# Low parts on VectorE, two weight pieces ahead and a later turn of the last queries, at the end of attention in a two-layer trunk

## The chip, the cores and the metric

One core of one Trainium2 chip. The metric is the device time of one execution in microseconds; before the change three runs gave 866.49, 868.11 and 872.79 us, median 868.11 us. Engines are named as in the profile: PE (matmul; PEld is its weight load), DVE, ACT, POOL, and SP, which issues most of the loads.

## The reference

640 tokens of width 1024 (512 latent, 128 context) pass two layers: gated grouped-query attention (16 query heads, 4 key heads of 64) and a gated linear recurrence in both directions. What matters here is the end of layer 0 and what its modulation needs:

```python
sh_s, sc_s, g_s = _adaln(c, ada_w[i], ada_b[i])      # SiLU(c) @ ada_w[i] + ada_b[i], cut in three
q = _rms_norm(q.reshape(B, L, N_HEADS, HEAD_DIM), q_gain)
...
p = jax.nn.softmax(s, axis=-1)
return jnp.einsum('bkgqs,bskd->bqkgd', p, vf).astype(q.dtype)
...
gated = o.reshape(B, L, ATTN_WIDTH).astype(jnp.float32) * jax.nn.silu(g.astype(jnp.float32))
return gated.astype(o.dtype) @ w_out
...
xs = _layer_norm(DEEPNORM_ALPHA * xs + g_s * out_s, ln_gain[i], ln_bias[i])
```

## The kernel before, in words

**High and low parts.** Products of activations and weights are made from two fp32r parts of each operand: the high part is a rounded copy made on ACT, the low part the difference of the value and its high part, made by one subtraction on DVE or POOL. A product is then three matmuls: high by high, high by low, low by high. `split_piece` (L220) does this for a weight piece of 128x1024 (ACT copy L225, subtraction L226 on the engine that it is given), `split_act` (L947) for one of the eight 128x640 slices of the gated attention output `gs` (copy L948 into `hhi`, subtraction L949 into `hlo`).

**Loads.** Weight pieces of 512 KB come in one fixed `order` (L370 to L384), issued by `pump` (L199) on SP so that at most `RAW_AHEAD = 5` pieces are loaded and not yet split, in a ring of six buffers. In that order the seven last adaLN chunks (`ADA_B[3]`, two pieces each) come first, and then the eight pieces of attention's output weight `attn_w_out` (two column halves nh of four pieces i).

**Attention's weave.** `att_gen` sweeps four key heads ("chunks" c of 4 query heads and 256 columns). Of each unit (one head, 256 queries) the front makes scores on PE (`sc`, L732 and L733), their negated maximum on DVE (`nm`, L826), the exponential with its sum on ACT (`p`, L829), and two steps later the reciprocal on DVE (`rc`, L833) and the scaling on POOL (`p`, L834). Two units later the back turns p on PE (`pt`, L841), copies it out of PSUM (`pts`, L737, on ACT and DVE), and multiplies by the values (`pot`, L759), which DVE gates into `gs` (L764). A second generator runs beside it, one step for every 0.85 of its steps at most (`weave`, `Side`): the next chunk's queries (`q_gen`, L600: projection `qmm`, root mean square, rotary tables, high and low part `qs` on ACT and DVE, turn by PE `qps` L589, copy into X), mixed with adaLN chunks (`adaps` L266; row to columns L289; sums into `shsc` and `gcol` on DVE, L297 and L300). Behind chunk 3's queries stand, in this order: the last seven adaLN chunks (once chunk 3's backs have begun), the first two pieces of the output weight (`prefetch_gen`, L959), and the split of the first six slices of `gs` (`split_gs(range(6))`). All this stands in one block whose instructions a list scheduler reorders within each engine.

**After the block** (L993 on, in program order save for what the code marks with `high_priority` or pins): the split of the last two slices (L1067), the other six output weight pieces (L1069), the first recurrence weights (`rhi`, `rlo`), and then the output projection `outp` (L1005, L1008, L1009) of five token tiles in the order (0,0), (1,0), (0,1), (1,1), (2,0) and so on of (tile, column half), 24 matmuls each. Both halves of one tile lie in one PSUM tile of two banks. After each half, `Norm.part` (L1026) reads it on DVE: a product with the gate (`y`, L1030), the residual (L1031), statistics (L1033).

The low parts stand on these engines before: `qs` and the recurrence's weights on DVE; `hlo` on POOL (L953); output weight pieces in turn, even i on POOL and odd i on DVE (L944).

Of the kernel before, what the change touches and what calls it, by code (L numbers as in the profile page):

```python
# [132 lines left out]
def hybrid_step(ctx: ExitStack, tc: tile.TileContext, a: dict, o: dict):  # L133
    nc = tc.nc
# [62 lines left out]
    order = deque()  # L197
# [22 lines left out]
    def split_piece(hi, lo, src, lo_eng=None, pinned=False):  # L220
        pump()
        got, raw = ahead.popleft()
        assert got == src, (got, src)
        pin = tc.keep_in_program_order if pinned else lambda ins: ins
        pin(nc.scalar.copy(hi, raw))  # L225
        pin((lo_eng or nc.gpsimd).tensor_tensor(lo, raw, hi.bitcast(F32), ALU.subtract))  # L226
        pump()
# [84 lines left out]
    def ada_gen(chunks):  # L312
        todo, last = None, None
        for l, c in chunks:
            ps = bank1("adaps")
            both = [take((f"ada_w{l}", c, i)) for i in range(2)]
            for i in (1, 0):
                ada_part(ps, i, both[i], 1)
            yield
            if last:  # L320
                last()
            last = todo and ada_out(*todo)
            yield
            todo = (l, c, ada_row(ps))
        if last:
            last()
        if todo:
            last = ada_out(*todo)
            yield
            if last:  # L330
                last()
                yield
# [25 lines left out]
    def pieces(name, c, n=2):  # L358
        return [(name, c, i) for i in range(n)]

    PIECES = [(nh, i) for nh in range(2) for i in range(4)]
# [5 lines left out]
    def ada_pieces(part):  # L367
        return [p for l, c in part for p in pieces(f"ada_w{l}", c)]
# [4 lines left out]
    for c in range(3):  # L373
        order.extend(pieces("attn_w_in", c + 1))
        order.extend(ada_pieces(ADA_B[c]))
    order.extend(ada_pieces(ADA_B[3]))
    order.extend(("attn_w_out", nh, i) for nh, i in PIECES)
    order.extend(("rec_w_in", h, i) for h in range(RH) for i in range(5))
    order.extend(("rec_w_out", nh, i) for nh, i in OUT1)
    for n, back in ((0, 2), (1, 1)):  # L380
# [17 lines left out]
    hhi = hp.tile([P, KT, NT], F32R, tag="hhi", name="hhi")  # L398
    hlo = hp.tile([P, KT, NT], F32R, tag="hlo", name="hlo")
# [100 lines left out]
    gs = gsp.tile([P, KT, NT], F32, tag="gs", name="gs")  # L500
# [76 lines left out]
    def q_split(r, tt0, n, odd, X, alloc):  # L577
        s2 = prep.tile([P, 1024], F32R, tag="s2", name="qs2", bufs=2)
        rv = view(r, 0, [[HD, 4 * n], [1, HD]])
        hv = view(s2, HD * odd, [[P, 4 * n], [1, HD]])  # L580
        nc.scalar.copy(hv, rv)
        nc.vector.tensor_tensor(view(s2, HD * (1 - odd), [[P, 4 * n], [1, HD]]), rv, hv.bitcast(F32), ALU.subtract)

        def back(i):
            pt = alloc("qps")
            pr = pt[:].bitcast(F32R)
            for h in range(4):
                s = i * 512 + h * P
                nc.tensor.transpose(pr[:, h * P:(h + 1) * P], s2[:, s:s + P], identr)  # L589
            c0 = (tt0 + i) * P  # L590
            nc.scalar.copy(X[:, :, c0:c0 + P], pt[:].rearrange("p (a b) -> p a b", a=4))  # L591
        return back
# [7 lines left out]
    def q_gen(c, X):  # L600
        w = Weights("attn_w_in", c, (nc.vector, nc.vector))
        yield
        yield
        pend = None
        for tt0, n in UNITS:
            ps = yield from tok_unit(w, tt0, n, "qmm")
            rstd = rms_stat(ps, n)
            yield
            if pend:
                for i in range(pend[1]):  # L610
                    pend[0](i)
                    yield
            else:
                yield
            yield
            qn = rms_apply(ps, n, rstd)
            r = rope_apply(qn, tt0, n, cosq, sinq, qg)
            yield
            pend = (q_split(r, tt0, n, c % 2, X, bank1), n)
        yield  # L620
        for i in range(pend[1]):
            pend[0](i)
            yield
# [191 lines left out]
    back_of = [0]  # L815
# [95 lines left out]
    side = Side()  # L911
# [27 lines left out]
    def wo_gen(layer, pieces, wpool):  # L939
        for nh, i in pieces:  # L940
            hi = wpool.tile([P, 1024], F32R, tag=f"wohi{nh}{i}", name="wohi")
            lo = wpool.tile([P, 1024], F32R, tag=f"wolo{nh}{i}", name="wolo")
            wo[nh, i] = tuple(t[:].rearrange("p (k n) -> p k n", k=2) for t in (hi, lo))
            split_piece(hi, lo, ("attn_w_out" if layer == 0 else "rec_w_out", nh, i), (nc.gpsimd, nc.vector)[i % 2])  # L944
            yield

    def split_act(dst_hi, dst_lo, src, eng=None):  # L947
        nc.scalar.copy(dst_hi, src)  # L948
        (eng or nc.vector).tensor_tensor(dst_lo, src, dst_hi.bitcast(F32), ALU.subtract)  # L949

    def split_gs(ks):
        for k in ks:
            split_act(hhi[:, k, :], hlo[:, k, :], gs[:, k, :], nc.gpsimd)  # L953
            yield

    ws = ExitStack()
# [2 lines left out]
    def prefetch_gen():  # L959
        wb.close()  # L960
        pq.close()
        wr.append(lpool("wr", 2))
        woa.append(ws.enter_context(pool("woa", 1)))
        yield from wo_gen(0, PIECES[:2], woa[0])

    def q_next(c):
        Xs[c] = xq[c % 2].tile([P, 4, NT], F32R, tag="X", name=f"X{c}")
        yield from q_gen(c, Xs[c])

    def mixed(q, ada):  # L970
        owed = 0.0
        for _ in q:
            yield
            owed += MIX
            while owed >= 1.0:
                owed -= 1.0
                if next(ada, True) is None:
                    yield
        yield from ada

    for c in range(1, 4):
        side.items.append((f"q{c}", mixed(q_next(c), ada_gen(ADA_B[c - 1])), lambda c=c: front_of[0] >= c - 1))
    side.items.append(("a", ada_gen(ADA_B[3]), lambda: back_of[0] == 3))
    side.items += [("w", prefetch_gen()), ("s", split_gs(range(6)), lambda: back_of[0] == 3)]
    weave(att, side, SIDE_B)
    side.finish()
    ph.close()
# [226 lines left out]
    norms = {}  # L1214
    for tt, nh in ((0, 0), (1, 0), (0, 1), (1, 1), (2, 0), (2, 1), (3, 0), (3, 1), (4, 0), (4, 1)):
        if nh == 0:
            norms[tt] = Norm(0, tt)
        out_mms(norms[tt].ps[nh], tt, nh, hhi, hlo)
        norms[tt].part(nh, norms[tt].ps[nh])
        if nh == 1:  # L1220
            with tc.high_priority() if tt == TS else nullcontext():
                norms[tt].finish()
            if tt > 1:
                h1_tile(tt - 1, norms[tt - 1].y)
            elif tt == 1:
                h1_tile(0, norms[0].y)
# [267 lines left out]
    side = Side(("t", tail_gen()))  # L1494
# [9 lines left out]
    for tt in range(TT):  # L1504
# [7 lines left out]
        else:  # L1512
            w = D // parts
            for n in range(parts):
                nh, c = divmod(n * w, 512)
# [86 lines left out]
```

## Time and profile before

| | |
|---|---|
| median of three runs | 868.11 us (866.49 to 872.79) |
| the profiled execution's own time | 868.67 us |
| its span, first to last instruction | 866.9 us, 19259 instructions |
| PE busy | 827.0 us (95%) |
| DVE / ACT / POOL busy | 528.8 / 382.5 / 205.9 us |
| mean granted TensorE clock | 0.992 |
| chain that ended last | PE 83%, DVE 5%, ACT 4%, issue 4%, DMA 3%, POOL 1% |

A busy row gives microseconds and share of the span. A row of waits names the engine and line that stood idle, behind what, for how long in all, how often and the longest. A timeline row gives start, duration, engine, line, operation, output and inputs, shape and count, and in brackets the idle time before it with what ended it; equal instructions in a row are merged, and a merged matmul's duration is the time from its first start to its last end. A row of windows gives the stretch in us, busy time (and instructions) of PE, PEld, DVE, ACT and POOL, the granted clock of TensorE (1.00 is full), the share of DMA and GB/s.

### The profile page before, as it was taken

The numbers are of one execution on the slowest core, as the hardware profiler recorded it, in microseconds if no ns is written. First come the engines' busy times: TensorE is split into PE (matmuls) and PEld (weight loads), VectorE is DVE, ScalarE is ACT, GpSimd is POOL, SyncE is SP. The second block draws the span as 40 slices with busy tenths as digits, with TensorE's granted clock in tenths as the row PEclk, the third lists the DMA queues.
The fourth block names the chain that finished last, engine by engine and source line by source line (L and its number), as shares of the span: only waits on it lengthen the run. The fifth ranks groups of instructions, "written<-read, shape, count | busy, mean of one in ns | idle before, by whom it ended". The sixth has DMA issues, their size and how long they took to land.

```text
span 866.9 us, 19259 instructions
## 1 busy us (share of the span) xinstructions
PE 827.0 (95%) x8124; PEld 739.7 (85%) x8124; DVE 528.8 (61%) x942; ACT 382.5 (44%) x756; POOL 205.9 (24%) x247
## 2 busy tenths in 40 slices
PE   5989999999999898989999999999999999999996
PEld 3669999778778766667899999999999999998886
DVE  3447535665846664567635666675848495867558
ACT  2222536554745754503244444444443454544332
POOL 0113001413414743600000040323324040502011
PEclk9999999999999999999999999999999999999999
DMA  9922112212212046251221232232224232322023
GB/s 358 411 88 86 55 68 74 99 50 99 98 49 99 1 161 229 88 228 74 83 73 50 82 96 83 79 105 70 85 68 123 62 99 81 98 74 93 8 97 122
DMA packets 29606, 89.86 MB, mean 104 GB/s; under 512 B 4336, under 2 KB 8944, under 8 KB 28496
## 3 DMA queue, kind: packets, MB, share of 16 engines
q1 hardware_dynamic: 19728, 73.08, 23.8%
q0 software_dynamic: 3168, 9.31, 3.9%
q10 hardware_dynamic: 6624, 6.24, 2.3%
q8 instruction: 64, 1.05, 0.5%
q14 instruction: 22, 0.18, 0.1%
HBM read 79.44 MB, written 9.18 MB: 102 GB/s over the span
## 4 chain that ended last, share of the span: by engine, by line
PE 83%; DVE 5%; ACT 4%; issue 4%; DMA 3%; POOL 1%; SPq 0%; ACTq 0%; DVEq 0%; POOLq 0%
PE rps L1147 7%; PE rps L1149 7%; PE rps L1148 6%; PE vgps L1137 5%; PE vgps L1139 4%; PE vgps L1138 4%; PE pot L759 4%; PE pt L841 4%; PE outp L1005 3%; PE outp L1009 2%; PE outp L1008 2%; PE adaps L266 2%; PE gps L337 2%; PE lv L1285 2%; PE gps L338 2%
## 5 line engine op out<-in xcount | busy, mean ns | idle before, releaser
L1147 PE MATMUL rps<-h1hi,rhi 128*128 128x320 f32 x368 | 118.3, 321 | 0.0
L1148 PE MATMUL rps<-h1lo,rhi 128*128 128x320 f32 x368 | 113.5, 308 | 0.0
L1149 PE MATMUL rps<-h1hi,rlo 128*128 128x320 f32 x368 | 113.4, 308 | 0.0
L226 DVE TENSOR_TENSOR rlo<-raw,rhi 128x1024 fp32r<-128x1024 f32 x32 | 44.1, 1380 | 46.0 <-ACT rhi L225 46.0
L834 POOL TENSOR_SCALAR p<-p,rc 128x640 f32<-128x640 f32 x64 | 53.2, 836 | 78.5 <-DVE rc L833 68.9
L1147 PEld LDWEIGHTS rps<-h1hi,rhi 128*128 128x128 f32 x368 | 69.2, 188 | 1.3
L1148 PEld LDWEIGHTS rps<-h1lo,rhi 128*128 128x128 f32 x368 | 69.3, 188 | 0.0
L1149 PEld LDWEIGHTS rps<-h1hi,rlo 128*128 128x128 f32 x368 | 69.1, 188 | 0.1
L829 ACT ACTIVATE p<-sc,nm 128x640 f32<-128x640 f32 x64 | 51.1, 799 | 35.4 <-DVE nm L826 29.1
L826 DVE TENSOR_REDUCE nm<-sc 128x1 f32<-128x640 f32 x64 | 51.6, 817 | 18.6 <-PE sc L733 17.9
L225 ACT CAST rhi<-raw 128x1024 fp32r<-128x1024 f32 x32 | 33.6, 1050 | 61.0 <-PE rps L1148 57.1
L1258 ACT COPY kc<-A 128x640 f32<-128x640 f32 x40 | 32.4, 811 | 52.0 <-PE lv L1285 29.7
L841 PE MATMUL pt<-ident,p 128*128 128x128 f32 x320 | 50.6, 283 | 3.2 <-ACT pts L737 1.5
L1137 PE MATMUL vgps<-rhi,h1hi 128*128 128x256 f32 x180 | 51.2, 284 | 0.0
L1138 PE MATMUL vgps<-rlo,h1hi 128*128 128x256 f32 x180 | 50.5, 280 | 0.0
L1139 PE MATMUL vgps<-rhi,h1lo 128*128 128x256 f32 x180 | 50.2, 279 | 0.0
L737 ACT COPY pts<-pt 128x512 f32<-128x512 f32 x64 | 36.6, 588 | 27.8 <-PE pt L841 27.5
L841 PEld LDWEIGHTS pt<-ident,p 128*128 128x128 f32 x320 | 37.7, 146 | 12.5 <-issue 8.9
L194 POOL TENSOR_TENSOR rstdo<-rs_t,mhalf 128x5 f32<-128x5 f32 x8 | 9.5, 1192 | 162.3 <-DVE rs_t L193 162.3
L732 PE MATMUL sc<-kk,X 128*128 128x320 f32 x128 | 42.8, 344 | 2.9 <-ACT p L829 2.8
L1137 PE MATMUL vgps<-wspare,h1hi 128*128 128x256 f32 x140 | 41.5, 297 | 0.0
L337 PE MATMUL gps<-hhi,whi 128*128 128x320 f32 x128 | 40.1, 313 | 0.7 <-ACT X L591 0.4
(273 smaller groups left out, 2413.2 us busy)
## 6 DMA issues: line engine op xcount, KB each, us to landing
raw<-in_rec_w_in SPq DMA_DIRECT2D x40, 512.0 KB, 4.0
raw<-in_ada_w SPq DMA_DIRECT2D x32, 512.0 KB, 3.9
raw<-in_ada_w SPq DMA_DIRECT2D x8, 1024.0 KB, 10.8
raw<-in_attn_w_in SPq DMA_DIRECT2D x16, 512.0 KB, 4.7
raw<-in_attn_w_out SPq DMA_DIRECT2D x8, 512.0 KB, 5.9
raw<-in_rec_w_out SPq DMA_DIRECT2D x8, 512.0 KB, 3.7
h<-in_xT SPq DMA_DIRECT2D x8, 320.0 KB, 9.2
x1d<-y SPq DMA_DIRECT2D x5, 512.0 KB, 2.6
```

Of the source, the lines that this page charges most:

```text
L226: pin((lo_eng or nc.gpsimd).tensor_tensor(lo, raw, hi.bitcast(F32), ALU.subtract))
L337: nc.tensor.matmul(ps[:, :320], w.hi(k)[:, c], hhi[:, k, t], start=(k == 0), stop=False)
L826: nc.vector.tensor_reduce(nm[:, 0:1], sc[:, :, :320], AX.XY, ALU.max, negate=True)
L829: nc.scalar.activation(halves(p[:]), sc[:, :, :320], AF.Exp, bias=nm[:, 0:1], accum_out=su[:, 0:1])
L834: nc.gpsimd.tensor_scalar(p, p, rs[:, 0:1], 1.0, ALU.mult, ALU.mult)
L841: nc.tensor.transpose(pt[:, i * 256 + q * P:i * 256 + (q + 1) * P], ps[q][:, (k0 + i) * P:(k0 + i + 1) * P], ident)
L1137: nc.tensor.matmul(out, h1hi[:, k, t], hi, start=(k == 0), stop=False)
L1138: nc.tensor.matmul(out, h1hi[:, k, t], lo, start=False, stop=False)
L1139: nc.tensor.matmul(out, h1lo[:, k, t], hi, start=False, stop=(k == KT - 1))
L1147: nc.tensor.matmul(ps[:, j, :320], hi[:, k, :], h1hi[:, k, t], start=(k == 0), stop=False)
L1148: nc.tensor.matmul(ps[:, j, :320], hi[:, k, :], h1lo[:, k, t], start=False, stop=False)
L1149: nc.tensor.matmul(ps[:, j, :320], lo[:, k, :], h1hi[:, k, t], start=False, stop=(k == KT - 1))
```

## The change

The edits, all around the end of attention:

- `wo_gen` gives every low part of a weight piece to DVE, and `split_gs` gives `hlo` to DVE. With that POOL makes no low part any more: four pieces of `wolo` and eight of `hlo` go over.
- In the load order the first two output weight pieces stand ahead of the last seven adaLN chunks, and the generator that splits them (`prefetch_gen`) runs ahead of these chunks too, right behind chunk 3's queries.
- `q_gen` yields twice more ahead of the turn of its last unit, in chunks 1 to 3.
- `Norm.part` of the first two token tiles is issued with high priority.

```diff
     for c in range(3):
         order.extend(pieces("attn_w_in", c + 1))
         order.extend(ada_pieces(ADA_B[c]))
+    order.extend(("attn_w_out",) + p for p in PIECES[:2])
     order.extend(ada_pieces(ADA_B[3]))
-    order.extend(("attn_w_out", nh, i) for nh, i in PIECES)
+    order.extend(("attn_w_out",) + p for p in PIECES[2:])
...
             pend = (q_split(r, tt0, n, c % 2, X, bank1), n)
+        yield
+        yield
         yield
...
-            split_piece(hi, lo, ("attn_w_out" if layer == 0 else "rec_w_out", nh, i), (nc.gpsimd, nc.vector)[i % 2])
+            split_piece(hi, lo, ("attn_w_out" if layer == 0 else "rec_w_out", nh, i), nc.vector)
...
-            split_act(hhi[:, k, :], hlo[:, k, :], gs[:, k, :], nc.gpsimd)
+            split_act(hhi[:, k, :], hlo[:, k, :], gs[:, k, :])
...
+    side.items.append(("w", prefetch_gen()))
     side.items.append(("a", ada_gen(ADA_B[3]), lambda: back_of[0] == 3))
-    side.items += [("w", prefetch_gen()), ("s", split_gs(range(6)), lambda: back_of[0] == 3)]
+    side.items += [("s", split_gs(range(6)), lambda: back_of[0] == 3)]
...
-        norms[tt].part(nh, norms[tt].ps[nh])
+        with tc.high_priority() if tt < 2 else nullcontext():
+            norms[tt].part(nh, norms[tt].ps[nh])
```

What this does to the order of DVE's instructions at three places follows (in the rows of the change, lines after L617 carry numbers up to five higher).

DVE from the last gating of attention to the first sums of the output projection, before (`pot` is the product of probabilities and values, `wolo` and `rlo` are low parts of output and recurrence weights, `y` of the outp row is the gated output of tile 0):

```order
L764 TENSOR_TENSOR gs<-pot,gs 128x256
L993 UNCONDITIONAL_BRANCH
L226 TENSOR_TENSOR wolo<-raw,wohi 128x1024 x3
L226 TENSOR_TENSOR rlo<-raw,rhi 128x1024
L1074 TENSOR_TENSOR modA<-shsc_85,lnc 128x16
L1075 TENSOR_TENSOR modB<-shsc_85,lnc 128x16
L226 TENSOR_TENSOR rlo<-raw,rhi 128x1024
L1076 TENSOR_TENSOR modB<-modB,shsc_85 128x16
L1030 TENSOR_TENSOR y<-outp,gate_108 128x512
```

The same place with the change:

```order
L767 TENSOR_TENSOR gs<-pot,gs 128x256
L997 UNCONDITIONAL_BRANCH
L952 TENSOR_TENSOR hlo<-gs,hhi 128x640
L226 TENSOR_TENSOR wolo<-raw,wohi 128x1024
L952 TENSOR_TENSOR hlo<-gs,hhi 128x640
L226 TENSOR_TENSOR wolo<-raw,wohi 128x1024 x5
L1034 TENSOR_TENSOR y<-outp,gate_108 128x512
L1078 TENSOR_TENSOR modA<-shsc_85,lnc 128x16
L1079 TENSOR_TENSOR modB<-shsc_85,lnc 128x16
L226 TENSOR_TENSOR rlo<-raw,rhi 128x1024
```

Two `hlo` and three more `wolo` came in, and the first read of `outp` moved ahead of both recurrence weights.

DVE in the last adaLN chunks, some 25 us earlier, before (`row` and `gcol` are an adaLN chunk's sums as a row and as columns):

```order
L764 TENSOR_TENSOR gs<-pot,gs 128x256
L280 COPY row<-adaps 128x256
L226 TENSOR_TENSOR wolo<-raw,wohi 128x1024
L826 TENSOR_REDUCE nm<-sc 128x1 x2
L300 TENSOR_TENSOR gcol_83<-adaps_3794,small 128x4
```

With the change:

```order
L767 TENSOR_TENSOR gs<-pot,gs 128x256
L280 COPY row<-adaps 128x256
L829 TENSOR_REDUCE nm<-sc 128x1 x2
L300 TENSOR_TENSOR gcol_83<-adaps_3814,small 128x4
L280 COPY row<-adaps 128x256
```

The low part of the output weight piece is gone from between the row and the maxima.

DVE while chunk 3's last queries are made, before (`qs` is the low part of the queries, `ss` the sum of their squares):

```order
L826 TENSOR_REDUCE nm<-sc 128x1
L833 RECIPROCAL rc<-su 128x1
L297 TENSOR_TENSOR shsc_85<-adaps_3231,small 128x4
L826 TENSOR_REDUCE nm<-sc 128x1
L582 TENSOR_TENSOR qs_3203<-r,qs_3203 128x8x64
```

With the change:

```order
L829 TENSOR_REDUCE nm<-sc 128x1
L952 TENSOR_TENSOR hlo<-gs,hhi 128x640
L836 RECIPROCAL rc<-su 128x1
L952 TENSOR_TENSOR hlo<-gs,hhi 128x640
L297 TENSOR_TENSOR shsc_85<-adaps_3231,small 128x4
L952 TENSOR_TENSOR hlo<-gs,hhi 128x640 x2
L829 TENSOR_REDUCE nm<-sc 128x1
L583 TENSOR_TENSOR qs_3203<-r,qs_3203 128x8x64
```

Four low parts of `gs` stand between two maxima that followed each other with two short instructions between them. A little later two `wolo`, with another `hlo` ahead of them, stand around the maximum of chunk 3's context scores, and on ACT the two high parts of these pieces stand behind the copy of the last turned queries and ahead of two copies `pts`.

## The prediction

> **What bounds the kernel now.** I read the busy times first, then PE's waits around the change, then the stretches of 4 us in which these fall, and then the rows of each wait in order of time. The first row of the page:
>
> ```profile
> PE 827.0 (95%) x8124; PEld 739.7 (85%) x8124; DVE 528.8 (61%) x942; ACT 382.5 (44%) x756; POOL 205.9 (24%) x247
> ```
>
> PE is busy for 827.0 of 866.9 us, so only its idle time, about 40 us, and time at a lower clock can be won. PE's waits between 270 and 420 us, the stretch that the change touches:
>
> ```profile
> PE outp L1005 <- DVE y L1030: 4.2, 2, 3.8
> PE qps L589 <- DVE qs L582: 2.7, 1, 2.7
> PE adaps L289 <- DVE gcol L300: 2.6, 1, 2.6
> PE sc L732 <- ACT p L829: 0.9, 4, 0.3
> PE outp L1005 <- DVE gs L764: 0.5, 1, 0.5
> ```
>
> Three waits, all for DVE, make most of it: 2.7 us for the last queries, 2.6 us for adaLN columns, 3.8 us for the first sums of the output projection. The windows (columns: stretch, busy PE, PEld, DVE, ACT, POOL, clock, DMA):
>
> ```profile
> 284.00:288.00 4.00, 3.92 (x34) 3.67 (x32) 1.79 (x5) 4.00 (x9) 4.00 (x4) 1.00 0.00 0
> 296.00:300.00 4.00, 1.67 (x17) 1.69 (x17) 1.81 (x5) 2.47 (x7) 2.85 (x3) 1.00 0.01 4
> 332.00:336.00 4.00, 2.20 (x25) 1.23 (x23) 2.37 (x3) 1.60 (x3) 2.15 (x1) 1.00 0.87 300
> 338.38:341.78 3.40, 3.40 (x17) 3.36 (x18) 1.10 (x3) 1.30 (x3) 0.79 (x2) 0.50 0.87 310
> 368.00:372.00 4.00, 0.23 (x2) 0.17 (x2) 3.97 (x7) 0.00 (x0) 0.64 (x1) 1.00 1.02 412
> 372.20:375.60 3.40, 3.40 (x10) 2.68 (x9) 2.91 (x5) 0.00 (x0) 0.00 (x0) 0.55 0.88 319
> ```
>
> Behind the second and the third wait PE runs for 3.4 us at a granted clock of 0.50 and 0.55; behind the first it stays at 1.00. So two of the waits cost more than their length.
>
> **What a low part costs.** Rows of single tiles and groups (least, median and most ns; then mean):
>
> ```profile
> L226 DVE TENSOR_TENSOR rlo<-raw,rhi x32: 1209/1222/3392, 366.3 to 776.4; 128x1024 fp32r<-128x1024 f32 x32
> L226 DVE TENSOR_TENSOR wolo<-raw,wohi x4: 1597/2248/3436, 333.6 to 363.0; 128x1024 fp32r<-128x1024 f32 x4
> L460 DVE TENSOR_TENSOR hlo<-h,hhi x8: 815/826/1362, 11.5 to 58.0; 128x640 fp32r<-128x640 f32 x8
> L949 POOL TENSOR_TENSOR hlo<-gs,hhi x8: 1542/1569/2587, 284.8 to 359.4; 128x640 fp32r<-128x640 f32 x8
> L225 ACT CAST wohi<-raw x6: 1041/1044/1048, 355.9 to 361.3; 128x1024 fp32r<-128x1024 f32 x6
> ```
>
> On DVE the same subtraction takes 1.22 us, but 2.25 us where POOL makes low parts beside it. Four `wolo` and eight `hlo` that go over cost DVE 4 x 1.22 + 8 x 0.826 = 11.5 us in all, and those already there get shorter.
>
> **The output projection's wait.** Rows in order of time:
>
> ```profile
> 356.25 0.50 PE L1005 MATMUL outp<-wohi,hhi 128*128 128x512 f32 x1 [0.53 <-DVE gs L764]
> 358.61 7.79 DVE L226 TENSOR_TENSOR wolo<-raw,wohi 128x1024 fp32r<-128x1024 f32 x3 [2.41 <-ACT wohi L225]
> 361.92 6.71 POOL L226 TENSOR_TENSOR wolo<-raw,wohi 128x1024 fp32r<-128x1024 f32 x2
> 366.33 3.39 DVE L226 TENSOR_TENSOR rlo<-raw,rhi 128x1024 fp32r<-128x1024 f32 x1
> 369.81 1.21 DVE L226 TENSOR_TENSOR rlo<-raw,rhi 128x1024 fp32r<-128x1024 f32 x1
> 371.03 0.68 DVE L1030 TENSOR_TENSOR y<-outp,gate 128x512 f32<-128x512 f32 x1
> 371.86 0.47 PE L1005 MATMUL outp<-wohi,hhi 128*128 128x512 f32 x1 [3.77 <-DVE y L1030]
> 376.28 0.39 PE L1005 MATMUL outp<-wohi,hhi 128*128 128x512 f32 x1
> 378.62 0.39 PE L1008 MATMUL outp<-wolo,hhi 128*128 128x512 f32 x1
> ```
>
> Tile 0's first half, 24 matmuls from 356.25 at 0.234 us (the last two rows' pace), is ready at about 362, yet DVE reads it at 371.03, behind five slow subtractions; PE's second half of the same tile waits for that read. With the change DVE starts at the last gating's end, about 356.2, with two `hlo` and six `wolo`: 2 x 0.83 + 6 x 1.22 = 9.0 us, to 365.2; the read ends at 365.9. PE wants it at 368.1, so 2.2 us of slack hide it. ACT's six high parts are unchanged, and the second of them is wanted by PE, as its 20th matmul, at about 360.7 with its low part, which DVE has by 356.2 + 2 x 0.83 + 2 x 1.22 = 360.3. Next late would be the read of tile 1's first half, behind two `rlo` (2.4 us) and tile 0's other two instructions: about 371.4, wanted at 373.6. So 3.77 us go. The clock: twelve matmuls from 371.86 to 376.28 take 4.42 us, ten at full clock from 376.28 to 378.62 2.34 us, so twelve 2.81; 1.6 us more go. **Term: 5.4 us.** Low end 0: DVE at 2.25 us for each `wolo` would be done at 372; POOL makes nothing there, so I stay at 1.22.
>
> **The adaLN columns' wait.**
>
> ```profile
> 328.89 1.09 PE L841 MATMUL pt<-ident,p 128*128 128x128 f32 x8
> 329.91 1.07 PE L266 MATMUL adaps<-raw,sil 128*32 128x256 f32 x16
> 331.05 0.42 DVE L280 COPY row<-adaps 128x256 f32<-128x256 f32 x1 [1.62 <-PE adaps L266]
> 333.63 1.60 DVE L226 TENSOR_TENSOR wolo<-raw,wohi 128x1024 fp32r<-128x1024 f32 x1 [2.16 <-ACT wohi L225]
> 333.76 0.44 PE L841 MATMUL pt<-ident,p 128*128 128x128 f32 x2
> 335.16 1.54 DVE L826 TENSOR_REDUCE nm<-sc 128x1 f32<-128x640 f32 x2
> 336.82 0.61 PE L289 MATMUL adaps<-small,row 128*128 128x2 f32 x4 [2.62 <-DVE gcol L300]
> 338.33 1.92 PE L841 MATMUL pt<-ident,p 128*128 128x128 f32 x8
> 339.91 0.61 PE L732 MATMUL sc<-kk,X 128*128 128x320 f32 x1
> ```
>
> DVE stands 2.16 us behind a `wolo` whose high part comes late, makes it in 1.60 us, and only then the maxima and the column sum that frees PE's bank. With both pieces made earlier, the maxima start when their scores are there (by my estimate 332, since PE makes them behind the product that ends at 330.98), and the column sum ends 1.54 + 0.15 us later at about 333.7, before PE, done at 334.20, asks for it. Then the last row (by 334.3) and a copy `pts` (0.4 us) are what PE can wait for: 0.3 us. So 2.3 us go. The clock: eight transposes take 1.58 us from 338.33 to 339.91 and 1.02 us from 328.89 to 329.91; 0.56 in 1.58, so 1.2 us in 3.40. **Term: 3.5 us**; ends 0 (the copies on ACT take the wait's place) and 4.3 (whole wait and half of 3.40 us).
>
> *A rule that would cut this term:* the Trainium skill, "TensorE: Matmul & The Clock Gate", Part 1, has the clock fall to half after an idle window of about 3.4 us and says to avoid gaps longer than that; by it a gap of 2.62 us costs no clock and the sum would be 1.2 us smaller. The trace differs: a granted clock of 0.50 from 338.38 on, behind a gap of 2.62 us.
>
> **The last queries' wait.**
>
> ```profile
> 287.11 5.02 POOL L949 TENSOR_TENSOR hlo<-gs,hhi 128x640 fp32r<-128x640 f32 x3
> 290.67 1.49 DVE L193 TENSOR_SCALAR rs_t<-ss 128x4 f32<-128x4 f32 x1
> 293.65 1.01 POOL L194 TENSOR_TENSOR rstd<-rs_t,mhalf 128x4 f32<-128x4 f32 x1
> 297.38 0.80 DVE L582 TENSOR_TENSOR qs<-r,qs 128x256 fp32r<-128x256 f32 x1
> 298.33 0.52 PE L589 MATMUL qps<-identr,qs 128*128 128x128 f32 x4 [2.72 <-DVE qs L582]
> ```
>
> POOL's three `hlo` hold its queue until 292.13; DVE's tiny `rs_t` ends just then (292.16), and `rstd` comes 1.5 us later behind two scalings. With the change POOL is free for `rstd`, but four `hlo` (3.3 us) stand in DVE's queue ahead of a maximum; DVE idles 4.00 - 1.79 = 2.2 us in 284 to 288, so the maximum, and with it the scores and the first turns, come 1.1 us later. Following the new order: `rs_t` at 292.2, `rstd` by 293, `qs` by about 296. PE, 1.1 us later and with four more transposes of probabilities (0.5 us) in front, comes to the turn at about 297 and finds it ready: 1.3 us earlier than now, and 0.5 us of work is done besides. The two yields move no more than that: on PE the turn stands in both orders behind ten transposes and ahead of ten. Against this, the two high parts (2 x 1.04 us) stand on ACT between the turned queries' copy and two copies `pts` for which the value products wait; the first of these is there about 0.6 + 2.1 + 0.6 = 3.3 us behind the turn, and the work that PE has before (ten transposes and two sets of scores) is by my estimate 2.8 us, so 0.5 us is lost. 1.3 + 0.5 - 0.5: **Term: 1.3 us**; ends -2.1 (the wait stays and both high parts are paid) and 2.7 (the wait goes whole).
>
> **What costs nothing.** The two early loads go to SP's queue ahead of 14 adaLN pieces. SP runs five pieces ahead and the DMA share is 0.00 in 284 to 288, so both lie ready when their high parts are made, and the adaLN pieces behind them are loaded five ahead as before; were they late, ACT would stand behind them and the turn's copies with it, which is the low end above. POOL has no low part left and only gains. The stretch after 392 us is PE at full clock in both.
>
> **The sum.** 5.4 + 3.5 + 1.3 = 10.2 us. The profiled execution took 868.67 us, 0.56 above the median of 868.11: 868.67 - 10.2 = **858.5 us**. A per cent is 8.7 us, about what a measurement of this kernel can tell from no change.
>
> **Rivals.** *Only the output projection gains.* DVE's queue is longer in attention, and the two other waits are replaced by others of their size: the maxima 1.1 us late, copies on ACT behind two high parts. For it: both are one wait each in a chain through DVE, ACT and POOL, with four waits of scores for `p` already there; against it: DVE is busy 1.79 and 2.37 of 4 us at these places. 868.67 - 5.4 = 863.3.
>
> *The clock falls once all the same.* A gap half as long as a window of 3.4 us was enough at 338.38, and not at 296; if one of the new small waits falls so, 1.2 us come back, 859.7.
>
> *More.* Without POOL's low parts all of DVE's chain gets shorter and the small waits (0.9 for `p`, 0.5 for `gs`) go too: 5.4 + 4.3 + 2.7 + 1.4 = 13.8, 854.9.
>
> *Slower.* The place is DVE's and ACT's queue between 284 and 302 us. If it is the path there, all that moves into it is paid: 5 x 0.826 + 2 x 1.22 + 2 x 1.04 = 8.7 us, and the idle PE falls to half clock for 3.4 us, 1.7 more: 10.4, while the first wait stays. Against 8.9 us of the other two: 868.67 + 1.5 = 870.2. It decides once DVE has no idle time left beside the four `hlo`; the 2.2 us there speak against it. The Trainium skill, "SBUF — State Buffer", "Who interferes with whom", speaks for it: a DVE instruction with two inputs in SBUF and a POOL instruction that reads SBUF shut each other out, whole instructions at a time, so seven moved subtractions could each meet a scaling by POOL (0.8 us), up to 5.6 us on top. The trace agrees that they meet (2.25 against 1.22 us); but before, POOL's subtractions met DVE's in the same way and longer.
>
> **How the numbers follow.** Forecast 0.43, only the projection 0.26, the clock 0.11, more 0.13, slower 0.07. Range: below, "more" is taken in to 854.5; above, "only the projection" and a microsecond of new waits to 864.5. Faster by over 1% (under 859.4): three quarters of the forecast, all of "more", a third of the clock's: 0.50. Slower by over 1% (over 876.8) needs the slower rival with its doubled price: 0.03. Within: 0.47.
>
> **What would show it.** Right: no PE wait for `y` at the first second half, `wolo` on DVE near 1.22 us, clock 1.00 throughout 284 to 380; no wait for `gcol`; the turn's wait under 1 us. Wrong: a PE gap over 1 us for `pts`, `nm` or `p` between 288 and 305, or a window at 0.5. Most of all the prediction fails if the wait for `y` has only changed its releaser.

## The result, and the profile after

| | before | after |
|---|---|---|
| median | 868.86 us (866.49 to 872.79, 5 executions) | 856.58 us (854.92 to 860.59, 5 executions) |
| ratio | | 0.9862, 95% interval 0.9824 to 0.99 |
| profiled execution | 868.67 us | 860.59 us, the longest of its five |
| its span | 866.9 us | 858.6 us |

The time lies 1.9 us under the forecast of 858.5 and inside its range. A ratio of 0.9862 is faster by 1.4%; the interval runs from 1.0 to 1.8%.

PE's waits between 270 and 420 us, which before were led by 3.8 us for `y`, 2.7 for `qs` and 2.6 for `gcol` (columns: us in total, times, longest):

```profile
PE outp L1009 <- DVE y L1034: 1.7, 2, 1.3
PE sc L735 <- ACT p L832: 0.6, 3, 0.3
```

The waits for `qs` and `gcol` are gone, and the longest that is left is 1.3 us, again for `y`. The windows of the same places (stretch, busy PE, PEld, DVE, ACT, POOL, granted clock, DMA share, GB/s):

```profile
284.00:288.00 4.00, 4.00 (x35) 3.89 (x34) 4.00 (x9) 3.38 (x8) 1.34 (x1) 1.00 0.00 0
296.00:300.00 4.00, 3.60 (x31) 2.89 (x27) 3.38 (x8) 3.36 (x8) 1.55 (x3) 1.00 0.01 4
332.00:336.00 4.00, 4.00 (x44) 3.40 (x43) 2.82 (x9) 1.20 (x3) 0.00 (x0) 1.00 0.88 299
336.00:340.00 4.00, 4.00 (x35) 3.40 (x35) 2.23 (x6) 3.40 (x9) 2.31 (x3) 1.00 0.64 231
368.00:372.00 4.00, 2.72 (x13) 1.87 (x12) 3.33 (x6) 0.00 (x0) 0.00 (x0) 1.00 0.50 194
```

PE's busy time in them went from 1.67 to 3.60, from 2.20 to 4.00 and from 0.23 to 2.72 of 4 us, and the clock is 1.00 in all, where it had been 0.50 and 0.55 behind two of the waits. DVE is at 4.00 of 4.00 in 284 to 288, and so is PE: nobody waits for it there. The low parts, now all on DVE (least, median, most ns):

```profile
L226 DVE TENSOR_TENSOR wolo<-raw,wohi x8: 1215/1220/1226, 301.4 to 358.7; 128x1024 fp32r<-128x1024 f32 x8
L952 DVE TENSOR_TENSOR hlo<-gs,hhi x8: 806/817/826, 287.5 to 353.4; 128x640 fp32r<-128x640 f32 x8
```

Twelve subtractions came to DVE, and its busy time rose by 0.9 us only, from 528.8 to 529.7: the `wolo` already there went from a median of 2.25 us to 1.22.

**Three stages instead of the whole time.** The four starts below cut the place of the change into stages: A from the turn of chunk 3's queries to an adaLN product, C from there to the first product of the output projection, D from there to the first product of the recurrent projection. Before, the two in the middle were at 329.91 and 356.25; the outer two:

```profile
276.50 0.46 PE L589 MATMUL qps<-identr,qs 128*128 128x128 f32 x4
422.69 0.28 PE L1137 MATMUL vgps<-rhi,h1hi 128*128 128x256 f32 x1
```

After:

```profile
279.11 0.46 PE L590 MATMUL qps<-identr,qs 128*128 128x128 f32 x4
330.59 1.07 PE L266 MATMUL adaps<-raw,sil 128*32 128x256 f32 x16
351.51 0.50 PE L1009 MATMUL outp<-wohi,hhi 128*128 128x512 f32 x1 [0.53 <-DVE gs L767]
413.52 0.28 PE L1141 MATMUL vgps<-rhi,h1hi 128*128 128x256 f32 x1
```

| stage | before | after | gained | predicted |
|---|---|---|---|---|
| A, last queries | 53.41 | 51.48 | 1.93 | 1.3 |
| C, adaLN columns | 26.34 | 20.92 | 5.42 | 3.5 |
| D, output projection | 66.44 | 62.01 | 4.43 | 5.4 |
| sum | 146.19 | 134.41 | 11.78 | 10.2 |

The two spans differ by 8.3 us only, not by 11.78. The profiled execution of after is 2.61 us late already at its first anchor (279.11 against 276.50), which lies ahead of every edit but the added `yield` in chunks 1 and 2, and 0.87 us are lost behind 422.69 (444.2 us to the span's end before, 445.1 after; 443.6 in another execution of the changed kernel). The first goes with the clock (windows of after, columns as above):

```profile
46.00:54.00 8.00, 7.52 (x51) 4.40 (x49) 3.68 (x7) 1.46 (x2) 0.34 (x1) 0.79 0.19 70
184.00:190.00 6.00, 4.75 (x26) 3.73 (x28) 4.49 (x10) 2.66 (x5) 1.49 (x2) 0.76 0.55 178
```

In the execution of before both stretches had 1.00. The clock lost in them is by my estimate worth up to 3.1 us (0.21 x 8 + 0.24 x 6); other kernels with the same added `yield` lost none there (last section). So the comparison of two profiled spans errs by some microseconds here; the stages and the medians (868.86 - 11.78 = 857.1, measured 856.58) agree.

### The profile page after: what moved, and what is told of

The parts are those of the page before. It is cut to its first block, busy times and chain, and to the rows that moved or that the text cites. A ratio compares the mean times of both kernels' runs of the same rounds, so it can differ in the third digit from the quotient of the medians.

```text
span 858.6 us, 19267 instructions
## 1 busy us (share of the span) xinstructions
PE 825.5 (96%) x8124; PEld 738.8 (86%) x8124; DVE 529.7 (62%) x954; ACT 381.5 (44%) x756; POOL 181.8 (21%) x235
## 4 chain that ended last, share of the span: by engine, by line
PE 83%; DMA 7%; DVE 4%; ACT 3%; issue 2%; POOL 0%; SPq 0%; DVEq 0%; ACTq 0%; POOLq 0%
PE rps L1151 7%; PE rps L1153 7%; PE rps L1152 7%; PE vgps L1141 5%; PE vgps L1143 4%; PE vgps L1142 4%; PE pot L762 4%; PE pt L844 4%; PE outp L1009 3%; PE outp L1013 3%; PE outp L1012 3%; PE gps L337 2%; PE lv L1290 2%; DMA h<-in_xT 2%; PE gps L338 2%; PE gps L339 2%
## 5 line engine op out<-in xcount | busy, mean ns | idle before, releaser
L837 POOL TENSOR_SCALAR p<-p,rc 128x640 f32<-128x640 f32 x64 | 55.2, 867 | 86.3 <-DVE rc L836 69.4
L226 DVE TENSOR_TENSOR rlo<-raw,rhi 128x1024 fp32r<-128x1024 f32 x32 | 42.0, 1311 | 46.0 <-ACT rhi L225 46.0
```

What stands on the lines that cost most here:

```text
L837: nc.gpsimd.tensor_scalar(p, p, rs[:, 0:1], 1.0, ALU.mult, ALU.mult)
```

## The experiments

The comparisons give a ratio to the kernel before, on the same chip. The kernel before took 868.86, 869.87, 869.24, 870.22 and 869.84 us beside the five groups of runs, so medians of different groups can differ by a microsecond for the same kernel. The stages tell more: A and C repeat to a few hundredths of a microsecond where nothing in them was changed, D of the changed kernel to 0.4 us:

| kernel | A | C | D | median us | ratio, 95% interval |
|---|---|---|---|---|---|
| before | 53.41 | 26.34 | 66.44 | 868.86 | |
| after | 51.48 | 20.92 | 62.01 | 856.58 | 0.9862 (0.9824 to 0.99) |
| after, once more | 51.46 | 20.92 | 61.62 | 857.86 | 0.9854 (0.9835 to 0.9874) |
| before + low parts on DVE | 51.23 | 25.52 | 60.92 | 861.62 | 0.9914 (0.9885 to 0.9944) |
| before + loads ahead | 54.35 | 20.92 | 66.44 | 864.56 | 0.9949 (0.9928 to 0.997) |
| before + later turn | 53.29 | 26.85 | 66.42 | 871.18 | 1.0004 (0.9983 to 1.0024) |
| before + early first reads | 53.41 | 26.40 | 60.89 | 864.97 | 0.9945 (0.9922 to 0.9969) |
| after + `x` asked for early | 51.46 | 20.92 | 60.40 | 855.40 | 0.9834 (0.9808 to 0.986) |
| after, no early first reads | 51.46 | 20.92 | 61.24 | 856.49 | 0.985 (0.9825 to 0.9874) |
| after, `hlo` back on POOL | 53.16 | 20.92 | 63.06 | 860.39 | 0.9891 (0.9866 to 0.9915) |
| after, turn not later | 50.64 | 21.44 | 61.27 | 857.82 | 0.9858 (0.9832 to 0.9883) |
| after, half of `wolo` on POOL, no early reads | 51.46 | 20.92 | 65.21 | 862.53 | 0.9909 (0.9892 to 0.9925) |
| after, half of `wolo` on POOL | 51.48 | 20.92 | 66.85 | 861.15 | 0.9898 (0.9881 to 0.9915) |
| after + `x` early, turn not later | 50.64 | 21.44 | 60.41 | 856.49 | 0.9834 (0.981 to 0.9857) |

Theory to begin with, by the prediction's terms: D is DVE's low parts or the order of its queue, C is the early low part, A is POOL set free. The rival: each wait has only found another releaser. Four kernels do one part of the change alone.

**Low parts on DVE alone.**

```diff
-            split_piece(hi, lo, (...), (nc.gpsimd, nc.vector)[i % 2])
+            split_piece(hi, lo, (...), nc.vector)
-            split_act(hhi[:, k, :], hlo[:, k, :], gs[:, k, :], nc.gpsimd)
+            split_act(hhi[:, k, :], hlo[:, k, :], gs[:, k, :])
```

> The kernel before with one edit: all low parts of output weight pieces and of the gated output on DVE. Theory (contention and queue length): DVE's six wolo take 1.22 us each, the first read of outp ends near 368.7 in the old time frame, PE's wait for y falls from 3.77 to under 1.3 us and the half clock behind it goes; the queries' wait for qs falls from 2.72 to under 1 us since POOL no longer holds rstd back; the adaLN wait for gcol stays at 2.6 us or grows by the one wolo that comes to DVE there, up to 3.9. In all 4 to 6 us faster, 863 to 865 us beside a before of 868.9. Rival (only the place in the queue counts, not the contention): wolo on DVE stay over 2 us or the wait for y stays over 3 us, and the time is within 2 us of before.

861.62 us, 8.25 under the 869.87 measured beside it. PE's waits of this kernel:

```profile
PE adaps L289 <- DVE gcol L300: 2.1, 1, 2.1
PE outp L1005 <- DVE y L1030: 0.7, 2, 0.4
```

A and D have their gains (2.18 and 5.52 us), and C keeps most of its wait: 2.1 us for `gcol`, 0.5 less than expected. The waits for `y` and `qs` do what the theory says, but the gain of 8.25 us is more than the 4 to 6 us expected (the stages add to 8.5).

**Loads ahead alone** (the hunks of the load order and of `side.items`).

> The kernel before with one edit: two output weight pieces loaded and split ahead of the last adaLN chunks, one of their low parts still on POOL. Theory (each place has its own cause): the wait for gcol (2.62 us) and the half clock behind it go, the wait for y stays at 3.8 us with its half clock, the wait for qs stays at 2.7 us; 4 to 5.5 us faster, about 864. Rival (the parts need each other): POOL's low part (2.4 us) in front of the scalings of p makes a new PE wait of over 1.5 us between 290 and 306, and less than 3 us are won.

864.56 us, as expected. PE's waits:

```profile
PE qps L590 <- DVE qs L583: 2.7, 1, 2.7
PE outp L1007 <- DVE y L1032: 4.2, 2, 3.8
```

No row for `gcol` any more, and the two other waits stand untouched. Stage C takes 20.92 us, to the hundredth what it takes in the changed kernel: this edit alone gives the whole gain of C, and the 0.82 us that the low parts alone gain there do not come on top. In A it costs 0.94 us.

**Later turn alone** (the two `yield`).

> The kernel before with one edit: the turn of the last queries two steps later. On PE four more transposes of probabilities (0.5 us) come to stand ahead of the turn. Theory: the wait for qs falls by these 0.5 us to 2.2, nothing else changes, the time is within 1 us of before. Rival (the later turn is what removes that wait): it falls under 1 us and 2 us are won.

Ratio 1.0004: nothing. The wait for `qs` is 1.8 us instead of 2.7 (2.2 expected), but in the same stage scores wait 0.4 us longer for `p` and transposes 0.3 us for `pts`, and A gains 0.12 us while C loses 0.51.

**Early first reads alone** (the high priority of `Norm.part` for two tiles; POOL keeps its low parts).

> The kernel before with one edit: the first read of outp ahead of both recurrence weights on DVE; POOL's low parts stay. Theory (queue order is enough at this place): the read ends near 367.1 in the old time frame, before PE asks at 368.1; PE's wait for y falls from 3.77 to under 1 us, the half clock behind it goes, 4 to 5.5 us faster, about 864. Rival (contention is what counts): low parts of the third and fifth piece, on POOL until 365.3 and 368.6, take the place of the wait, PE idles over 2 us for wolo or y, and less than 2.5 us are won.

864.97 us, as expected, and D is 60.89, as short as with the low parts on DVE. PE's waits:

```profile
PE adaps L289 <- DVE gcol L300: 2.6, 1, 2.6
PE outp L1005 <- DVE y L1030: 0.4, 1, 0.4
```

So D has two sufficient causes, and their gains (5.52 and 5.55 us alone) don't add. Both are larger than the 4.43 of the whole change, in which both are there: something new is late in the changed kernel. Its rows in order of time (a value in brackets is the idle time ahead and what ended it):

```profile
354.11 5.76 DVE L226 TENSOR_TENSOR wolo<-raw,wohi 128x1024 fp32r<-128x1024 f32 x5
359.79 0.68 DVE L1034 TENSOR_TENSOR y<-outp,gate 128x512 f32<-128x512 f32 x1
360.13 1.05 ACT L225 CAST rhi<-raw 128x1024 fp32r<-128x1024 f32 x1 [1.61 <-DMA raw<-in_rec_w_in]
360.14 1.09 ACTq L1024 DMA_DIRECT2D x<-in_xs  x2
361.78 1.22 DVE L226 TENSOR_TENSOR rlo<-raw,rhi 128x1024 fp32r<-128x1024 f32 x1
367.71 0.69 DVE L1035 SCALAR_TENSOR_TENSOR y<-x,y 128x512 f32<-128x512 f32 x1 [4.71 <-DMA x<-in_xs]
369.05 0.67 DVE L1034 TENSOR_TENSOR y<-outp,gate 128x512 f32<-128x512 f32 x1
369.77 0.50 PE L1009 MATMUL outp<-wohi,hhi 128*128 128x512 f32 x1 [1.28 <-DVE y L1034]
```

Tile 0 is read at 359.79, as planned. Its second instruction adds the residual `x`, and DVE stands 4.71 us for that; the read of tile 1's first half is queued behind it, and PE waits 1.28 us for that read. ACT asks for `x` only when it comes to the second `rhi`, for whose raw piece it waits itself. Three questions follow: is it `x`; does the queue's order still matter; what of A is `hlo`, what the turn?

**`x` asked for early.** To the changed kernel:

```diff
     drain(split_gs(range(6, 8)))
+    norms = {tt: Norm(0, tt) for tt in range(2)}
...
-    norms = {}
...
-        if nh == 0:
+        if tt not in norms:
             norms[tt] = Norm(0, tt)
```

> The changed kernel, but the two residual tiles x (for token tiles 0 and 1) are asked for ahead of the output weight pieces, not behind the first 24 products. Theory (what is left of the projection's wait is the residual tile that lands late: DVE stood 4.71 us for it in front of the read of tile 1's first half): DVE adds x without a wait, reads tile 1's first half by about 364, PE's 1.28 us wait for y is gone and nothing new stands there; from the first product to the first of the recurrent projection about 60.7 us where the changed kernel took 62.0, the time about 1.3 us under the changed kernel's 856.6, some 855.3. Rival (the low parts are still what is late: DVE's queue, not the load): the read of tile 1's first half comes no earlier, y's wait stays over 1 us, 856.6. Second rival: the two issues on ACT's queue (about 1.1 us each) push the six high parts back, and PE waits for a high or low part instead: 1 to 2 us slower, 858.

D is 60.40 us, 1.6 less than in the changed kernel; 855.40 us. The intervals of the two ratios overlap, so the gain is read from D. DVE's rows:

```profile
355.49 0.69 DVE L1034 TENSOR_TENSOR y<-outp,gate 128x512 f32<-128x512 f32 x1 [0.47 <-PE outp L1013]
357.23 0.69 DVE L1035 SCALAR_TENSOR_TENSOR y<-x,y 128x512 f32<-128x512 f32 x1
360.14 0.69 DVE L1034 TENSOR_TENSOR y<-outp,gate 128x512 f32<-128x512 f32 x1 [0.48 <-PE outp L1013]
```

Now DVE waits for PE at both reads, PE's longest wait for `y` is 0.4 us (at a later tile), and nothing stands at the addition of `x`. The scheduler also put the first read and the addition ahead of the last two `wolo`, so the order of DVE's queue changed with the edit. But by the changed kernel's own rows `x` is enough: without its 4.71 us the read of tile 1 would start at 364.3, and PE asks for it at 368.5 (369.77 - 1.28). (The two issues of `x` take 1.09 us together, not each as the second rival has it.)

**No early first reads** (the high priority taken out of the changed kernel).

> The changed kernel without the high priority of the first reads: all low parts on DVE, the loads ahead, the turn later. Theory (either the cheap low parts or the order of DVE's queue is enough, and they do not add): DVE reads tile 0's first half behind all six wolo and two rlo, 2 x 1.22 us later, the wait for y is some 0.5 to 2 us and the clock stays at 1.00; within 1 us of the changed kernel, ratio to before about 0.986 to 0.987. Rival (the order of the queue carries the gain): y's wait is back at 3 to 4 us with the half clock behind it, about 861, ratio about 0.991.

D is 61.24 and the longest wait for `y` 0.4 us: with cheap low parts the order of the queue is worth nothing here, where `x` is late; with `x` early it was not tried.

**`hlo` back on POOL** (in `split_gs`; the weights' low parts stay on DVE).

> The changed kernel with the eight low parts of the gated values back on POOL (the output weights' stay on DVE). Theory (what the last queries' turn gains comes from POOL being free for rstd): rs_t and rstd stand behind three hlo again, the turn waits about 2 us for qs, and the stretch from the last queries' turn to the columns of the last gate is about 1.5 to 2 us longer than the changed kernel's; the two other waits stay away; time about 858.3, ratio to before about 0.988. Rival (the turn's gain came from the loads or the two yields): no wait for qs over 1 us, 856.6, ratio 0.986.

860.39 us, 2 us above the time expected: A is back at 53.16 us, so 1.7 of its 1.93 us are `hlo`, but the wait for `y` did not stay away, and D is 63.06. PE waits for `qs` again, and DVE's small row shows why:

```profile
PE outp L1009 <- DVE y L1034: 2.6, 2, 2.1
PE qps L590 <- DVE qs L583: 1.8, 1, 1.8
```

```profile
291.10 1.50 DVE L193 TENSOR_SCALAR rs_t<-ss 128x4 f32<-128x4 f32 x1
297.82 0.81 DVE L583 TENSOR_TENSOR qs<-r,qs 128x256 fp32r<-128x256 f32 x1
```

The wait for `y` is taken up at the end of this section. In the changed kernel the same two DVE instructions take 0.15 and 0.47 us:

```profile
293.43 0.15 DVE L193 TENSOR_SCALAR rs_t<-ss 128x4 f32<-128x4 f32 x1
297.08 0.47 DVE L583 TENSOR_TENSOR qs<-r,qs 128x256 fp32r<-128x256 f32 x1
```

**Turn not later** (the two added `yield` taken out of the changed kernel).

> The changed kernel without the two added yields: the turn of the last queries stands two steps earlier in the walk. Theory (on PE the turn stands behind ten transposes and ahead of ten in both orders; the yields give nothing by themselves): the same within 0.5 us, 856.6, the wait for qs 0.2 to 1 us. Rival (the yields are what hides the chain rs_t, rstd, qs now): a wait for qs of 1.5 to 2.5 us, 858 to 859.

857.82 us, where the changed kernel had 856.58 and 857.86. PE has no wait for `qs` at all, where 0.2 to 1 us was expected, so the rival falls. Without the yields some PE work falls on the other side of the border between A and C (A has 422 matmuls and C 181, where the changed kernel has 427 and 177), so only their sum can be read: 72.08 against 72.40 us, 0.3 us to the worse by the yields, if anything.

**Half of `wolo` back on POOL**, without and with the early reads:

```diff
-            split_piece(hi, lo, (...), nc.vector)
+            split_piece(hi, lo, (...), (nc.gpsimd, nc.vector)[i % 2])
```

> The changed kernel with two parts undone at once: every second output weight piece's low part is back on POOL, and the first reads have no high priority. Left are the loads ahead, the gated values' low parts on DVE and the turn. Theory (the projection's wait goes by either of the two, so without both it is back whole, and the two other terms stay): y's wait 3 to 4 us with the half clock behind it, from the first product of the projection to the first of the recurrent projection about 66.4 us as in the kernel before; the stretches ahead of it as in the changed kernel (51.5 from the last queries' turn to the adaLN product, 20.9 from there to the first product of the projection); time about 861.5, ratio 0.991. Rival (it was the gated values' low parts, off POOL, that made DVE quick enough): y's wait stays under 2 us and the stretch under 63.

> The changed kernel with every second output weight piece's low part back on POOL, the high priority kept. Theory (the order of DVE's queue is enough by itself): y's wait 0.4 to 1.5 us although wolo on DVE takes 1.6 us and more beside POOL's; time within 1 us of the changed kernel's 856.6, ratio 0.986 to 0.987. Rival (POOL's two low parts of 2.4 to 3.4 us each are late for PE): a wait for wolo on POOL over 1 us, 858 to 859.

For the first the time is near what was expected (862.53) and the manner is not: the wait comes in two pieces, 2.3 us for a `wolo` and 1.6 us for `y`, with a granted clock of 1.00 behind both. In the second theory and rival fall: 861.15 us, D is as long as before the change (66.85 against 66.44), and the `wolo` that PE waits for is one of DVE's, not of POOL's. Rows in order of time:

```profile
350.21 2.51 DVE L952 TENSOR_TENSOR hlo<-gs,hhi 128x640 fp32r<-128x640 f32 x1 [0.67 <-ACT hhi L951]
352.64 7.87 DVE L226 TENSOR_TENSOR wolo<-raw,wohi 128x1024 fp32r<-128x1024 f32 x3
356.09 0.50 PE L1012 MATMUL outp<-wolo,hhi 128*128 128x512 f32 x1 [2.34 <-DVE wolo L226]
361.49 1.05 ACT L225 CAST rhi<-raw 128x1024 fp32r<-128x1024 f32 x1 [4.89 <-DMA raw<-in_rec_w_in]
370.53 0.50 PE L1009 MATMUL outp<-wohi,hhi 128*128 128x512 f32 x1 [1.82 <-DVE y L1034]
```

By these rows the early read is enough only while the gated values' low parts are made elsewhere. Here the last `hlo` stands in DVE's queue ahead of the three `wolo`, takes 2.51 us beside POOL's `wolo` instead of 0.82, and the `wolo`, 2.6 us each on average, are late for PE itself, 7 us after the projection's start. Moving `hlo` to DVE, which A needs, makes it necessary that POOL gives up `wolo` too. The change without any low part moved, that is the loads and the early reads together, was not run; the stages of these two edits alone (A and C of the one, D of the other) add to 136.2 us, 1.8 more than the changed kernel's. The Trainium skill, "SBUF — State Buffer", "Who interferes with whom", says that a DVE instruction with two inputs in SBUF and a POOL instruction that reads SBUF wait for each other; the 2.51 against 0.82 us agree.

The late low parts also hold the buffers of raw pieces: SP's queue (its waits, 348 to 372 us) stands for them, in this kernel

```profile
SPq L213 <- POOL wolo L226: 19.8, 1, 19.8
```

and in the changed one

```profile
SPq L213 <- DVE wolo L226: 23.0, 6, 18.6
```

(the longest waits reach back to the time ahead of the projection). By these rows the next weights, `rhi` and with it `x` come later the later a `wolo` is done; no run changes that alone.

**Both small gains together** (`x` early, no added `yield`).

> The residual tiles asked for early (as in the kernel that did only that to the changed one, 855.4) and the two added yields taken out again, which by the stretch ahead of the projection saved 0.3 us. Theory (small and independent): about 855, ratio 0.983; the stretch from the last queries' turn to the first product of the projection about 72.1 us, from there to the recurrent projection 60.4, no wait for y over 0.5 us. Rival (the turn's place moves other work against it): that stretch back above 72.4.

As expected by the stages: A and C 72.08, D 60.41, 1.9 us under the changed kernel, with 0.9834 again. The time is 1.5 us above the 855 expected; by the medians it is no faster than `x` early alone (856.49 against 855.40 us).

**The changed kernel once more.**

> The changed kernel once more, unchanged. Theory (what is left of y's wait is set by when the second piece of the recurrent weights lands, since ACT makes its high part before it asks for the residual tiles; that landing varies from one execution to the next): y's longest wait is anywhere from 0.4 to 1.3 us and goes with ACT's wait for that piece (0.97, 1.15 and 1.61 us in three executions so far gave 0.4, 0.4 and 1.3), the projection's stretch is 61.2 to 62.0 us, the two stretches ahead of it 51.5 and 20.9 again; time 856 to 857.5, ratio 0.985 to 0.986. Rival (the 1.28 us is part of the changed kernel's order and always there): 1.2 to 1.4 us again whatever ACT waits.

ACT's wait for the second raw piece and PE's wait for `y` here:

```profile
359.35 1.05 ACT L225 CAST rhi<-raw 128x1024 fp32r<-128x1024 f32 x1 [1.31 <-DMA raw<-in_rec_w_in]
368.86 0.51 PE L1009 MATMUL outp<-wohi,hhi 128*128 128x512 f32 x1 [0.85 <-DVE y L1034]
```

Four kernels that have the same order from the last gating on but for `hlo` (turn not later, this one, the changed one, `hlo` on POOL) give pairs of 0.97 and 0.45, 1.31 and 0.85, 1.61 and 1.28, 2.36 and 2.13 us: PE's wait goes up with the landing of that piece, microsecond for microsecond and a little more. The theory holds but for the time, 857.86 us, 0.4 above its upper end: what is left of the wait goes with a load, and it varies between executions of the same kernel (0.85 and 1.28 us).

## Why the prediction was right, point by point

**D, predicted 5.4, measured 4.43 (4.82 in the second execution).** The wait of 3.77 us and the half clock went as reckoned: tile 0's read ended 8.96 us behind the first product (359.79 + 0.68 - 351.51), reckoned 9.65, and the stage is 5.5 us shorter in the kernels in which nothing else comes late (60.92, 60.89; what still waits there for `y` is 0.4 us at most). The term was mis-sized by the step "Next late would be the read of tile 1's first half, behind two `rlo` (2.4 us) and tile 0's other two instructions: about 371.4, wanted at 373.6". That counted DVE's queue and not what an instruction in it waits for: the addition of `x` stood 4.71 us for a transfer. Before, `x` had 6.7 us from its issue until DVE came to it:

```profile
365.07 0.82 ACTq L1020 DMA_DIRECT2D x<-in_xs  x2
371.74 0.69 DVE L1031 SCALAR_TENSOR_TENSOR y<-x,y 128x512 f32<-128x512 f32 x1
```

With DVE 6.5 us earlier, counted from the first product, and the issue still behind ACT's second `rhi`, it had 2.9 (360.14 to 361.78 + 1.22). Asking for it early brings D to 60.40: the term would then be 6.0.

**C, predicted 3.5 with an upper end of 4.3, measured 5.42.** The mechanism is right, the loads ahead alone give it whole, and the size is too small. The windows of the whole stage, before

```profile
329.91:356.25 26.34, 22.20 (x177) 16.30 (x176) 10.58 (x25) 13.50 (x26) 7.90 (x7) 0.94 0.38 126
```

and after

```profile
330.59:351.51 20.92, 19.71 (x177) 14.79 (x176) 9.34 (x25) 10.87 (x24) 3.98 (x5) 1.00 0.31 110
```

have the same 177 matmuls on PE. Its idle time fell from 4.14 to 1.21 us, by 2.93: the whole 2.62 of `gcol`, of which I had left 0.3 to a new wait that did not come, and 0.3 of a wait for `pts` (0.48 to 0.17). Its busy time fell by 2.49 us, where my clock term had 1.2. The pace of full clock in that term came from a row of eight transposes at 1.02 us; in the changed kernel eight take 0.83 (335.39 to 336.22):

```profile
334.58 0.95 PE L289 MATMUL adaps<-small,row 128*128 128x2 f32 x8
335.39 1.07 PE L844 MATMUL pt<-ident,p 128*128 128x128 f32 x8
336.22 0.39 PE L735 MATMUL sc<-kk,X 128*128 128x320 f32 x1
```

With that pace the half clock of 3.40 us costs nearly its full half, 1.6 us (0.75 in 1.58). The cause of the remaining 0.9 us stays open: the groups of matmuls follow each other in another order (a group of scores and two transposes now stand behind the value products instead of ahead), and no run takes that apart.

**A, predicted 1.3, measured 1.93 and 1.95.** POOL set free was the right cause, 1.7 of it by the kernel with `hlo` back. `qs` came 2.9 us earlier than before, counted from the stage's start (297.08 - 279.11 = 17.97 against 297.38 - 276.50 = 20.88), where I had 296, 1.4 us earlier if that is its start and 2.2 if it is its end: on top of POOL's queue, `rs_t` itself fell from 1.49 to 0.15 us, which I had read as a symptom and not priced. No run separates the two, since both go with `hlo` on POOL. That the two yields "move no more than that" was about right (0.3 us the other way), and the moved subtractions and high parts have a price: 0.94 us where the loads alone are moved, with POOL still slowing DVE; I had 0.5.

**The sum and the rivals.** 10.2 predicted, 11.78 in the stages, 12.3 between the medians: C too small by 1.9, A by 0.6, D too large by 1.0. That the sum is off by only 1.6 us where the terms are off by 3.5 is luck in part, since D's error has the other sign. "Only the projection" and "slower" fell at once, since both other waits went. "The clock falls once all the same" didn't happen between 280 and 400. "More" had A and C together nearly right (7.0 us, measured 7.35; A was less and C more) and missed `x`. The small waits for `p` and `gs`, which "more" let go, stayed but for 0.3 us.

## What to carry to other kernels

When a read is pulled ahead in an engine's queue, go through every instruction between it and the next one that somebody waits for, and ask of each not only how long it takes but what it waits for: here a residual tile, whose load is issued by another engine behind work of its own. Two edits that each cure a wait by themselves don't add, but one can become necessary through a third: `hlo` on DVE paid only with `wolo` there too. And where the clock ahead of the change differs between two profiled executions, compare stages between fixed instructions, and not spans.

## What the runs showed that was not expected

**The same early code runs at full or half clock from one execution to the next.** At 46 to 54 and 184 to 190 us the changed kernel's execution had a mean clock of 0.79 and 0.76, in each for some 3.4 us at 0.50. The kernel with half of `wolo` on POOL (early reads kept), which is the same up to there, the added `yield` included, had

```profile
46.00:54.00 8.00, 7.06 (x54) 4.77 (x55) 5.26 (x10) 1.81 (x3) 1.43 (x2) 1.00 0.20 72
184.00:190.00 6.00, 5.25 (x44) 3.79 (x44) 3.68 (x9) 1.90 (x4) 1.01 (x1) 1.00 0.45 156
```

and came to the turn of chunk 3's queries at 276.46 us, the changed one at 279.11. Of the seven profiled executions with this code, three had 1.00 in both stretches and came to the turn at 276.3 to 276.9, four had 0.79 and 0.72 to 0.76 and came at 278.3 to 279.1. Of the last combined kernel's five executions one, at a mean clock of 0.997, took 851.47 us, three at 0.992 took 856.49 to 857.75. That spread of 6 us is several times the gain of either small edit (1.6 and 0.3 us by the stages), which is why their medians don't tell them apart.

**Whether a gap costs clock isn't told by its length here.** Behind PE's gap of 1.82 us (half of `wolo` on POOL, 370.53) the clock fell:

```profile
370.50:374.00 3.50, 3.47 (x11) 2.77 (x12) 2.81 (x5) 0.00 (x0) 0.00 (x0) 0.71 0.06 21
```

Behind gaps of 1.28 us in the changed kernel, of 2.33 and 1.60 in the one with half of `wolo` on POOL and no early reads, of 2.13 in the one with `hlo` on POOL and of 2.72 in the kernel before (298.33) it did not. Where the kernel before fell to 0.50, at 338.38, its gap was 2.62 us and PE idle for 1.85 of the 3.41 us ahead. The Trainium skill, "TensorE: Matmul & The Clock Gate", Part 1, has the clock fall after an idle window of about 3.4 us that is free-running. That like gaps end differently would fit a free-running window, but a whole idle one was not needed here, neither behind the 1.82 us nor behind the 2.62.

**A one-input instruction on 128x4 waits for POOL too.** `rs_t` took 1.49 and 1.50 us in the five kernels in which POOL made `hlo` beside it, and 0.14 to 0.16 us in the others. Before, it ended at 292.16 us, POOL's third `hlo` at 292.13.
